# Neighbourhood attention in a hybrid encoder layer: the bias laid out beside the gates and kept in DRAM, and weight low parts, output sums and gate products on VectorE

## The chip, the cores and the metric

The kernel runs on one core of a Trainium2 chip. The metric is the device time of one execution in microseconds (us). A profiled execution gives the trace; its span is the time from the first to the last instruction. The engines are called TensorE (PE in the profile, with PEld for its weight loads), VectorE (DVE), ScalarE (ACT) and GpSimd (POOL). SP issues the DMAs.

## The reference, cut to what matters

One layer, 1024 tokens and 16 meta tokens, width 1024. A combined projection feeds two groups: latent attention (MLA) and two-dimensional neighbourhood attention (NA). NA has 16 heads of 64; a token on a 16 x 64 grid looks at a clamped 8 x 16 window, with a learned bias by relative offset, and at the 16 meta tokens, with a bias of their own.

```python
        k_win = k_rows[:, :, col_idx]
        v_win = v_rows[:, :, col_idx]
        dr_idx = r0 + jnp.arange(win_r, dtype=jnp.int32) - r + (NA_WIN_R - 1)
        bias = rel_bias[:, dr_idx[None, :, None], dc_idx[:, None, :]]
        s_win = (jnp.einsum('bqhd,brqchd->bhqrc', q_row, k_win).astype(jnp.float32) * scale
                 + bias.astype(jnp.float32)[None])
        s_meta = jnp.einsum('bqhd,bmhd->bhqm', q_row, k_meta).astype(jnp.float32) * scale + meta_b
        s = jnp.concatenate([s_win.reshape(B, NA_HEADS, GRID_W, n_win), s_meta], axis=-1)
        p = jax.nn.softmax(s, axis=-1).astype(v.dtype)
...
        y_na = _na(na_q, na_k, na_v, na_q_norm_w[l], na_k_norm_w[l],
                   na_rel_bias[l], na_meta_bias[l]) * jax.nn.silu(g_na)
        h_res = h_res + jnp.concatenate([y_mla, y_na], axis=-1) @ w_out[l]
```

q and k are normalised by head before this (QK-norm).

## The kernel before, in words

A float32 operand x is held as two parts in the matmul's type, a high part (a cast by ScalarE, such as wnh or hT) and a low part (x minus the high part, such as wnl or hTl). A product is then three matmuls: high x high, high x low, low x high. The helper that makes a low part is `lo_of`, one line of it (L104) being the operation of all of them; `mm` (L107) is every matmul, `tr` (L110) every transpose on TensorE. `bank` hands out PSUM banks by tag; s and tr share four, acc and o have two each.

The work stands in five stages, by time of the span:

- 0 to 190 us: the gates. 16 blocks of 128 gate columns, each for two halves of the tokens; a gate is 24 matmuls of 128x512. Weights come in groups gr of three blocks (`g_load`), four tiles of 128x2x384, into six buffers; the low parts of a tile are two operations on POOL. After each of the six gates of gr 3, `bias_rows` makes up to three of the 16 grid rows of `base`, the bias before it is laid out by window: two matmuls (rbh and rbl are the parts of the bias table, selr a selection matrix) and one VectorE operation. base then goes to DRAM as base_d.
- 190 to about 700 us: NA, 8 pairs of heads (p), each in 8 steps (t) of 128 tokens. The loop over g runs the projection of step g + 6 (`part`, in three pieces), the transposes of q and k of step g + 3 (`na_tr`), scores of step g + 1 (`na_qk`), the transposes of the probabilities of step g (`na_ptr`), and the products with v of step g - 1 (`na_pv`). `na_meta` projects the meta tokens of a pair at its step t=0. After every second step `na_pv` adds up the two banks of outputs into y_na; after every fourth `na_sum` and `na_fin` divide by the softmax sums and multiply by the gate.
- Behind the last pair's projections the same loop runs the projection of the latent keys and values (`lat_nat`, natl), whose norm is on POOL.
- Up to 1160 us: MLA. Then the output projection.

TensorE runs in the order in which the code is written. The other queues (VectorE, ScalarE, POOL and SP) are put in order by a scheduler, so code that is moved can move instructions of all of them; within a queue, an instruction that waits holds all behind it.

QK-norm goes through `na_norm`: sums of squares, then `rstd`, in which POOL does a pow (L93) and VectorE one Newton step (L94, L95, L97), then raw x rs_y (L467). The transposes of `na_tr` read raw. `na_bias` loads a pair's base rows and lays them out as bi (inner steps), b0 and b7 (first and last step) with 11 operations, on POOL for p > 0. `na_load` loads a pair's weights; all eight low parts are on POOL for p > 0:

```python
        d["w"] = w_load(lambda k: w_na[p, :, 2 * k:2 * k + 2, :], 384, (G, G if p else V), True)
```

G, V, S and T are POOL, VectorE, ScalarE and TensorE. In the outputs ScalarE copies both halves out of PSUM (u_na and u2_na) and POOL adds them; rx, kvm and u2_na share one buffer (tag ux).

Of the kernel before, what the change touches and what calls it, by code (L numbers as in the profile page):

```python
# [48 lines left out]
def hybrid_layer(ctx, tc, x, x_t, meta, meta_t, norm_w, w_na, w_g, w_lat, lat_w, w_uq, w_ukv, vec128, qpe_w, kpe_w,  # L49
# [375 lines left out]
    def na_bias(p):
        d = st[p]
        E = G if p else V
        bs = np2.tile([P, 2, NB * ROWS], F32, name="bs", bufs=1)
        nc.sync.dma_start(bs, base_d[2 * p:2 * p + 2].rearrange("h p n -> p h n"))
        bi = np2.tile([P, 2, WI], F32, name="bi")  # L430
        b0 = np2.tile([P, 2, WE], F32, name="b0", bufs=1)
        b7 = np2.tile([P, 2, WE], F32, name="b7", bufs=1)
        mb = metab[:, 2 * p:2 * p + 2, :]
        im = imask[:, None, :].to_broadcast([P, 2, WI])
        E.tensor_copy(b0[:, :, 0:128], bs[:, :, 128:256])
        E.tensor_copy(b0[:, :, 128:144], mb)
        E.tensor_copy(b0[:, :, 144:272], bs[:, :, 256:384])
        for o, bb, w in ((0, 0, 128), (144, 8, 128), (288, 16, 112)):
            E.tensor_tensor(bi[:, :, o:o + w], bs[:, :, bb * 16:bb * 16 + w], im[:, :, o:o + w], op=ALU.add)
        E.memset(bi[:, :, 128:144], MASK)  # L440
        E.tensor_copy(bi[:, :, 272:288], mb)
        E.tensor_copy(b7[:, :, 0:128], bs[:, :, 0:128])
        E.tensor_copy(b7[:, :, 128:144], mb)
        E.tensor_copy(b7[:, :, 144:272], bs[:, :, 128:256])
        d["bi"], d["b0"], d["b7"] = bi, b0, b7
# [849 lines left out]
```

## Time and profile before

| | us |
|---|---|
| median of 3 runs | 1372.32 (1371.27 to 1373.38) |
| the profiled execution's own time | 1372.07 |
| its span | 1370.3 |
| busy TensorE / VectorE / ScalarE / POOL in the span | 1310.3 / 924.6 / 833.7 / 568.5 |

TensorE is busy 96% of the span, but a busy TensorE is not always at full clock, and the share is an average over stages. The granted clock is 0.985 on average. Pairs are told apart by the first matmul of a pair's meta projection; pair 1 starts at 232.27 us, pair 6 at 532.28.

### The profile page before, as it was taken

How to read it: one execution, taken by the hardware profiler on the slowest of the kernel's cores; microseconds unless marked ns; L12 is line 12 of the kernel's file. 1: busy time of each engine (PE TensorE's matmuls, PEld its weight loads, DVE VectorE, ACT ScalarE, POOL GpSimd, SP SyncE). 2: the span in 40 equal slices, each digit the busy share in tenths (PEclk: the TensorE clock that was granted, in tenths of full speed). 3: DMA queues.
4: the chain of work that ended last, by engine and by line, in shares of the span. 5: the costliest groups of instructions: out<-in, count | busy, mean ns of one | idle time of the engine just before them, and what ended most of it. 6: DMA issues, size and time to landing. Idle time of an engine off the chain costs nothing.

```text
span 1370.3 us, 24834 instructions
## 1 busy us (share of the span) xinstructions
PE 1310.3 (96%) x8116; PEld 1212.9 (89%) x8116; DVE 924.6 (67%) x2957; ACT 833.7 (61%) x2319; POOL 568.5 (41%) x1057
## 2 busy tenths in 40 slices
PE   9999999999999989999789789999999999999999
PEld 7888889989898988999789789999999999988887
DVE  4923236877877877788648898988997998641110
ACT  6622136778787877788756567777777777630110
POOL 4312145465654746364445545724734652000000
PEclk9999999999999999999999899999999999999999
DMA  9342551221212213120201110100010022254231
GB/s 341 124 141 87 182 149 38 57 84 43 74 51 66 62 55 99 45 67 28 59 16 48 43 36 17 40 28 21 33 31 25 30 80 75 81 166 130 73 109 46
DMA packets 81968, 102.03 MB, mean 74 GB/s; under 512 B 10279, under 2 KB 60839, under 8 KB 81719
## 3 DMA queue, kind: packets, MB, share of 16 engines
q1 hardware_dynamic: 81839, 100.45, 23.4%
q8 instruction: 64, 1.05, 0.3%
q14 instruction: 65, 0.53, 0.1%
HBM read 70.01 MB, written 24.12 MB: 69 GB/s over the span
## 4 chain that ended last, share of the span: by engine, by line
PE 74%; DVE 14%; ACT 6%; issue 3%; POOL 2%; DMA 1%; SPq 0%; DVEq 0%; ACTq 0%; POOLq 0%
PE ps_acc L107 21%; PE mps_acc L107 11%; PE ps_s L107 9%; PE mps_s L107 8%; PE mps_st L107 7%; PE mps_o L107 5%; PE ps_o L107 5%; PE mps_tr L110 4%; PE ps_tr L110 4%; DVE m_sb L967 1%; DVE rs_y L97 1%; DVE rs_t L95 1%; DVE PT L104 1%; DVE mPT L104 1%; DVE rs_t L94 1%
## 5 line engine op out<-in xcount | busy, mean ns | idle before, releaser
L107 PE MATMUL ps_acc<-wnh,hT 128*128 128x384 f32 (+1 forms) x560 | 205.0, 366 | 6.0 <-DVE natl L666 5.5
L107 PE MATMUL ps_acc<-wnh,hTl 128*128 128x384 f32 (+1 forms) x560 | 188.8, 337 | 0.0
L107 PE MATMUL ps_acc<-wnl,hT 128*128 128x384 f32 (+1 forms) x560 | 188.5, 337 | 0.0
L93 POOL TENSOR_TENSOR rs_y<-rs_v,mhalf 128x1 f32<-128x1 f32 (+5 forms) x170 | 148.7, 878 | 75.2 <-DVE rs_v L89 52.9
L104 POOL TENSOR_TENSOR wnl<-wnf,wnh 128x384 fp32r<-128x384 f32 (+3 forms) x132 | 122.7, 954 | 104.9 <-ACT wnh L151 85.9
L107 PE MATMUL mps_s<-mkT,mq 128*128 128x346 f32 (+1 forms) x576 | 132.2, 338 | 1.3 <-DVE mPT L104 0.9
L107 PEld LDWEIGHTS ps_acc<-wnh,hT 128*128 128x128 f32 x560 | 107.2, 191 | 7.8 <-DVE natl L666 6.0
L561 ACT ACTIVATE s_sb<-s_sb,nmn 128x400 f32<-128x400 f32 (+1 forms) x128 | 77.0, 602 | 55.2 <-DVE nmn L559 54.5
L107 PEld LDWEIGHTS ps_acc<-wnl,hT 128*128 128x128 f32 x560 | 107.4, 192 | 0.0
L993 ACT CAST mPT<-mps_tr 128x512 fp32r<-128x512 f32 x128 | 74.5, 584 | 54.1 <-PE mps_tr L110 53.1
L107 PEld LDWEIGHTS ps_acc<-wnh,hTl 128*128 128x128 f32 x560 | 106.5, 190 | 0.0
L107 PE MATMUL mps_o<-mPT,mV 128*128 128x256 f32 x768 | 106.1, 287 | 0.0
L967 DVE TENSOR_SCALAR_CACHE_REDUCE m_sb<-mps_s 128x346 f32<-128x346 f32 (+1 forms) x192 | 97.4, 512 | 9.6 <-PE mps_s L107 7.7
L104 DVE TENSOR_TENSOR mPT<-mps_tr,mPT 128x512 fp32r<-128x512 f32 x128 | 87.6, 686 | 13.2 <-ACT mPT L993 12.0
L107 PEld LDWEIGHTS mps_s<-mkT,mq 128*128 128x128 f32 x576 | 93.4, 192 | 3.0 <-DVE mPT L104 1.5
L107 PEld LDWEIGHTS mps_o<-mPT,mV 128*128 128x128 f32 x768 | 94.8, 189 | 0.2
L530 POOL CAST qs<-qz 64x128 fp32r<-64x128 f32 x128 | 40.5, 316 | 124.9 <-ACT qz L526 88.9
L104 DVE TENSOR_TENSOR PT<-ps_tr,PT 128x384 fp32r<-128x384 f32 (+2 forms) x160 | 72.3, 469 | 24.1 <-ACT PT L582 23.3
L976 ACT ACTIVATE m_sb<-m_sb,mnm 128x1040 f32<-128x1040 f32 x64 | 74.6, 1166 | 19.8 <-DVE mnm L975 14.0
L110 PE MATMUL mps_tr<-ident,m_sb 128*128 128x128 f32 x512 | 76.7, 273 | 2.4 <-DVE mq L104 1.0
L582 ACT CAST PT<-ps_tr 128x384 fp32r<-128x384 f32 (+2 forms) x160 | 61.7, 407 | 17.4 <-PE ps_tr L110 16.5
L107 PE MATMUL ps_o<-PT,Vt 128*128 128x256 f32 x256 | 61.4, 301 | 8.2 <-DVE PT L104 7.8
(465 smaller groups left out, 3815.9 us busy)
## 6 DMA issues: line engine op xcount, KB each, us to landing
wnf<-in_w_na_dram SPq DMA_DIRECT2D x32, 384.0 KB, 3.5
g_d<-g SPq DMA_DIRECT2D x32, 256.0 KB, 2.3
wnf<-in_w_out_dram SPq DMA_DIRECT2D x32, 256.0 KB, 2.7
wnf<-in_w_g_dram SPq DMA_DIRECT2D x19, 384.0 KB, 4.7
Vp<-Vt SPq DMA_DIRECT2D x48, 112.0 KB, 2.2
yfo<-y_d SPq DMA_DIRECT2D x24, 192.0 KB, 2.7
gt<-g_d SPq DMA_DIRECT2D x16, 256.0 KB, 3.5
y_d<-y_na SPq DMA_DIRECT2D x16, 256.0 KB, 2.2
```

Source lines behind the costliest of these rows:

```text
L93: G.tensor_tensor(y, v, mhalf[:np_, :n], op=ALU.pow)
L94: E.tensor_tensor(t, y, y, op=ALU.mult)
L95: E.tensor_tensor(t, t, v, op=ALU.mult)
L104: eng.tensor_tensor(dst, src, f(hi), op=ALU.subtract)
L107: T.matmul(o, lhsT=l, rhs=r, start=start, stop=stop, skip_group_check=True)
L110: T.transpose(out=o, in_=i, identity=ident[: i.shape[0], : i.shape[0]])
L530: G.tensor_copy(qs[h_, j], qz[l_, j])
L561: S.activation(sb, sb, AF.Exp, scale=-1.0, bias=mn, accum_out=d["sum", t // 4][:, t % 4, j:j + 1])
L582: S.copy(pt[:n, c0:c1, 0, :], ps[:n, c0:c1])
L967: V.tensor_scalar(st["sb", h, t][:, ks], s_ps, -SCALE, BIG, op0=ALU.mult, op1=ALU.min, accum_out=st["mx", h, t][:, b:b + 1])
L976: S.activation(sb, sb, AF.Exp, scale=-1.0, bias=nm, accum_out=st["ms", h, t // 2][:, t % 2:t % 2 + 1])
L993: S.copy(dh, ps)
```

## The change

Five things are changed.

1. The bias matmuls stand behind the gates of gr 2 instead of gr 3. A new `stage_bias` lays the bias of one pair out, on POOL, after each of the first eight gates of gr 3 and later, and stores it in DRAM (bias_d). In NA one load by pair (bo) replaces `na_bias`'s load and its 11 operations. The mask and the meta bias are loaded early.
2. The low parts of the weights of pairs 1 to 7 are made by VectorE, not POOL.
3. The output sums: ScalarE copies one half (u_na), VectorE adds the other half out of PSUM. The copies u2_na and POOL's sum are gone. rx, now with a buffer of its own, is copied by ScalarE.
4. The product of gate and softmax reciprocal (gt) is on VectorE.
5. `na_meta` stands at t=1 (before: t=0) and `na_meta_tr` at t=3 (before: t=2).

```diff
     for gr in range(2, 6):
         gw = g_load(gr)
         for b in range(min(3, 16 - 3 * gr)):
             for hf in (1, 0):
                 gate(3 * gr + b, gw, b * P, hf)
-                if gr == 3:
+                if gr == 2:
                     for k in range(3):
                         rk = (2 * b + hf) * 3 + k
                         if rk < ROWS:
                             bias_rows(rk)
-        if gr == 3:
-            nc.sync.dma_start(base_d.rearrange("h p n -> p h n"), base.rearrange("p h b r -> p h (b r)"))
-            sctx.close()
+                elif todo_b:
+                    stage_bias(todo_b.pop(0))
+    sctx.close()
...
+    def stage_bias(p):
+
+        E = G
+        bs = base[:, 2 * p:2 * p + 2].rearrange("p h b r -> p h (b r)")
+        bo = sg.tile([P, 2, WB], F32, name="sgb", bufs=3)
+        bi, b0, b7 = bo[:, :, :WI], bo[:, :, WI:WI + WE], bo[:, :, WI + WE:]
+        mb = metab[:, 2 * p:2 * p + 2, :]
+        im = imask[:, None, :].to_broadcast([P, 2, WI])
+        for o, bb, w in ((0, 0, 128), (144, 8, 128), (288, 16, 112)):
+            E.tensor_tensor(bi[:, :, o:o + w], bs[:, :, bb * 16:bb * 16 + w], im[:, :, o:o + w], op=ALU.add)
+        E.memset(bi[:, :, 128:144], MASK)
+        E.tensor_copy(bi[:, :, 272:288], mb)
+        for b_, c in ((b0, 128), (b7, 0)):
+            E.tensor_copy(b_[:, :, 0:128], bs[:, :, c:c + 128])
+            E.tensor_copy(b_[:, :, 128:144], mb)
+            E.tensor_copy(b_[:, :, 144:272], bs[:, :, c + 128:c + 256])
+        nc.sync.dma_start(bias_d[p], bo)
...
     def na_load(p):
         d = st[p] = {}
-        d["w"] = w_load(lambda k: w_na[p, :, 2 * k:2 * k + 2, :], 384, (G, G if p else V), True)
+        d["w"] = w_load(lambda k: w_na[p, :, 2 * k:2 * k + 2, :], 384, (V, V) if p else (G, V), True)
...
+        bo = np2.tile([P, 2, WB], F32, name="bo")
+        nc.sync.dma_start(bo, bias_d[p])
+        st[p].update(bi=bo[:, :, :WI], b0=bo[:, :, WI:WI + WE], b7=bo[:, :, WI + WE:])
...
                 o = d["o"][j].rearrange("p t (a n) -> p t a n", a=2)
                 S.copy(u[a], o[b])
-                S.copy(u2[a], o[a])
-            G.tensor_tensor(u, u, u2, op=ALU.add)
...
+                V.tensor_tensor(u[a], u[a], o[a], op=ALU.add)
+            V.tensor_tensor(y, u[:, :, 0, :], u[:, :, 1, :], op=ALU.add)
...
-        rx = np2.tile([P, 4, 2, 64], F32, name="rx", tag="ux", bufs=1)
-        G.tensor_copy(rx.rearrange("p t j d -> p (t j) d"),
-                      r.rearrange("p t j -> p (t j)")[:, :, None].to_broadcast([P, 8, 64]))
+        rx = np2.tile([P, 4, 2, 64], F32, name="rx", bufs=1)
+        S.copy(rx.rearrange("p t j d -> p (t j) d"),
+               r.rearrange("p t j -> p (t j)")[:, :, None].to_broadcast([P, 8, 64]))
...
-        G.tensor_tensor(gt, gt, rp, op=ALU.mult)
+        V.tensor_tensor(gt, gt, rp, op=ALU.mult)
...
             if t == 0:
+                na_alloc(p)
+            if t == 1:
                 na_meta(p)
...
-            if t == 2:
+            if t == 3:
                 na_meta_tr(p)
```

How this moves instructions is shown at three places. The first is TensorE's queue around the first gate of gr 2. ps_acc and ps_s are the PSUM banks of two gates, hT and hTl the parts of the normed tokens (92 and 94 the second half of the tokens, 91 and 93 the first), wnh and wnl those of the weights. Before, the gate's last matmuls are followed by the next gate:

```order
L107 MATMUL ps_acc<-hT_92,wnh 128x512
L107 MATMUL ps_acc<-hTl_94,wnh 128x512
L107 MATMUL ps_acc<-hT_92,wnl 128x512 [waits Pool_49]
L107 MATMUL ps_s<-hT_91,wnh 128x512 [waits PE_49,Activation_49]
L107 MATMUL ps_s<-hTl_93,wnh 128x512
```

In the changed kernel six bias matmuls stand between them:

```order
L108 MATMUL ps_acc<-hT_92,wnh 128x512
L108 MATMUL ps_acc<-hTl_94,wnh 128x512
L108 MATMUL ps_acc<-hT_92,wnl 128x512 [waits Pool_49]
L108 MATMUL ps_tr<-rbh,selr 128x384 [waits DMAHW3_49,DMAHW2_49,DMAHW4_49,DMAHW1_49,DMAHW5_49,DMAHW0_49,DMAHW6_49,DVE_49,DMAHW7_49,PE_49,Activation_49]
L108 MATMUL ps_tr<-rbl,selr 128x384 [waits DVE_49]
L108 MATMUL ps_o<-rbh,selr 128x384
```

The bias matmuls, with their waits for the table's loads and parts, have come forward by six gates, from behind the first gate of gr 3.

The second place is VectorE's queue in a pair of NA, from the Newton step of raw to the low parts of the next pair's weights. PT are the transposed probabilities, Vt the parts of v, bi the bias of an inner step, s_sb the scores. Before (a pair's steps t=1 and 2):

```order
L464 TENSOR_REDUCE ssn<-sqn 128x8
L104 TENSOR_TENSOR Vt<-ps_acc,Vt 128x128
L89 TENSOR_SCALAR rs_v<-ssn 128x8
L104 TENSOR_TENSOR kM<-ps_tr,kM 64x128 x2
L529 SCALAR_TENSOR_TENSOR qs<-ps_tr,qkw_na,qz_1618 64x128 x2
L94 TENSOR_TENSOR rs_t<-rs_y 128x8
L559 ISA s_sb,nmn<-ps_s,b_3905 128x272
```

In the changed kernel, the piece with two of the eight low parts of a pair:

```order
L96 TENSOR_TENSOR rs_t<-rs_t,rs_v 128x8
L105 TENSOR_TENSOR wnl<-wnf,wnh 128x384
L105 TENSOR_TENSOR PT_1737<-ps_tr,PT_1737 128x3x128
L105 TENSOR_TENSOR wnl<-wnf,wnh 128x384
L105 TENSOR_TENSOR PT_1739<-ps_tr,PT_1739 128x3x128
L620 TENSOR_TENSOR y_na<-u_na 128x256
L98 SCALAR_TENSOR_TENSOR rs_y<-rs_t,rs_y 128x8
L105 TENSOR_TENSOR kM<-ps_tr,kM 64x128 x2
```

The low parts (wnl) now stand between operations that TensorE waits for: PT, and the Newton step before raw.

The third place is POOL's queue in the gates. Before, twelve low parts of 128x384 (gr 3 and 4) and eight of 128x128 (gr 5) follow one another:

```order
L93 TENSOR_TENSOR rs_y<-rs_v,mhalf 128x1 x4
L93 TENSOR_TENSOR rs_y<-rs_v,mhalf 16x1
L104 TENSOR_TENSOR wnl<-wnf,wnh 128x384 x8
L349 TENSOR_TENSOR tabq<-cs,qpw 128x8x32 x4
L349 TENSOR_TENSOR tabk<-csm,kpw 16x32 x4
L349 TENSOR_TENSOR tabk<-cs,kpw 128x8x32 x4
L104 TENSOR_TENSOR wnl<-wnf,wnh 128x384 x12
L104 TENSOR_TENSOR wnl<-wnf,wnh 128x128 x8
```

In the changed kernel the last tile of gr 4 stands in the middle of the eighth bias block (sgb):

```order
L398 TENSOR_TENSOR sgb<-base,imask 128x2x128 x2
L398 TENSOR_TENSOR sgb<-base,imask 128x2x112
L399 MEMSET sgb 128x2x16
L400 COPY sgb<-metab 128x2x16
L105 TENSOR_TENSOR wnl<-wnf,wnh 128x384 x2
L402 COPY sgb<-base 128x2x128
L403 COPY sgb<-metab 128x2x16
```

Six whole blocks stand ahead of the two middle tiles of gr 4, and one and a half more between these and its last tile, so these low parts have moved behind the bias.

## Rows read from the trace of the kernel before

**Rows 1.** Busy time by stretch: us, each engine, clock, DMA share, GB/s.

```profile
232.27:289.40 57.13, 56.09 (x365) 53.53 (x363) 45.01 (x133) 47.50 (x140) 33.77 (x48) 1.00 0.22 61
532.28:593.73 61.45, 57.60 (x364) 55.35 (x363) 48.21 (x134) 48.14 (x142) 33.80 (x49) 0.97 0.20 63
232.27:593.73 361.46, 342.15 (x2169) 327.80 (x2168) 285.38 (x803) 287.01 (x841) 204.92 (x288) 0.98 0.21 63
645.00:712.00 67.00, 54.08 (x337) 50.39 (x337) 37.74 (x118) 42.10 (x126) 31.82 (x75) 0.90 0.13 38
900.00:1000.00 100.00, 99.55 (x746) 97.77 (x745) 87.48 (x344) 74.11 (x211) 52.75 (x136) 1.00 0.09 29
```

**Rows 2.** TensorE's waits in NA: us in total, times, longest.

```profile
PE ps_tr L110 <- DVE nmn L559: 14.4, 6, 2.7
PE ps_acc L107 <- DVE natl L666: 5.5, 2, 4.3
PE ps_tr L110 <- POOL rx L622: 4.8, 1, 4.8
```

**Rows 3.** Timeline of pair 6: start us, us, operation, [idle before].

```profile
537.49 4.36 POOL L104 TENSOR_TENSOR wnl<-wnf,wnh 128x384 fp32r<-128x384 f32 x4
539.53 1.47 DVE L467 TENSOR_TENSOR raw<-raw,rs_y 128x512 f32<-128x512 f32 x1
543.33 0.44 PE L110 MATMUL ps_tr<-ident,raw 128*128 128x128 f32 x2 [2.66 <-DVE nmn L559]
547.17 0.52 PE L107 MATMUL ps_acc<-wnh,hTl 128*128 128x384 f32 x1
```

**Rows 4.** VectorE's timeline in pair 5.

```profile
497.07 0.17 DVE L97 SCALAR_TENSOR_TENSOR rs_y<-rs_t,rs_y 128x8 f32<-128x8 f32 x1
498.01 0.69 DVE L467 TENSOR_TENSOR raw<-raw,rs_y 128x512 f32<-128x512 f32 x1
```

**Rows 5.** VectorE's groups in pair 5: busy us, mean ns, idle before.

```profile
L467 DVE TENSOR_TENSOR raw<-raw,rs_y 128x512 f32<-128x512 f32 x4 | 3.8, 949 | 0.1
L97 DVE SCALAR_TENSOR_TENSOR rs_y<-rs_t,rs_y 128x8 f32<-128x8 f32 x4 | 3.0, 744 | 0.1
L95 DVE TENSOR_TENSOR rs_t<-rs_t,rs_v 128x8 f32<-128x8 f32 x4 | 2.7, 666 | 0.1
L94 DVE TENSOR_TENSOR rs_t<-rs_y 128x8 f32<-128x8 f32 x4 | 1.7, 416 | 0.7 <-POOL rs_y L93 0.7
```

**Rows 6.** VectorE's groups in the whole span.

```profile
L104 DVE TENSOR_TENSOR y0l<-yf,y0h 128x384 fp32r<-128x384 f32 x4 | 2.1, 555 | 0.2 <-ACT y0h L940 0.2
L104 DVE TENSOR_TENSOR mPT<-mps_tr,mPT 128x512 fp32r<-128x512 f32 x128 | 87.6, 686 | 13.2 <-ACT mPT L993 12.0
```

**Rows 7.** Timeline of the end of NA.

```profile
701.18 1.26 POOL L608 TENSOR_TENSOR u_na<-u_na 128x512 f32<-128x512 f32 x1
```

**Rows 8.** Timeline in gr 2.

```profile
81.06 0.39 PE L107 MATMUL ps_s<-hT,wnh 128*128 128x512 f32 x1
86.50 0.39 PE L107 MATMUL ps_acc<-hT,wnh 128*128 128x512 f32 x1
88.56 0.56 DVE L104 TENSOR_TENSOR rbl<-rb,rbh 120x384 fp32r<-120x384 f32 x1 [2.50 <-ACT rbh L341]
```

**Rows 9.** POOL's groups in pair 5; timeline at gr 4's start.

```profile
L439 POOL TENSOR_TENSOR bi<-bs,imask 128x256 f32<-128x256 f32 x2 | 1.4, 731 | 0.0
L442 POOL COPY b<-bs 128x256 f32<-128x256 f32 x1 | 0.4, 412 | 0.0
...
146.70 0.39 PE L107 MATMUL ps_acc<-hT,wnh 128*128 128x512 f32 x1
148.22 0.88 DVE L379 TENSOR_SCALAR base<-ps_o,rmask 128x384 f32<-128x384 f32 x1
```

**Rows 10.** Timeline of POOL and VectorE in the MLA stage.

```profile
788.87 0.56 POOL L93 TENSOR_TENSOR rs_y<-rs_v,mhalf 128x1 f32<-128x1 f32 x1 [0.59 <-DVE rs_v L89]
788.90 0.43 DVE L871 TENSOR_TENSOR mqraw<-mqraw,rs_y 128x256 f32<-128x256 f32 x1
```

More of the change, by code (lines that the diff above doesn't have):

```diff
@@ L34 @@
 WE = 272
+WB = WI + 2 * WE
 KS = 144
@@ L74, in load_bc @@
         return t
-    base_d = dram.tile([16, P, NB * ROWS], F32, name="base_d")
+    bias_d = dram.tile([NPAIR, P, 2, WB], F32, name="bias_d")
     g_d = dram.tile([16, P, D], F32, name="g_d")
@@ L300, in hybrid_layer @@
         for b in range(3):
-            gs = gp.tile([P, 512], F32, name="gs", bufs=5)
+            gs = sp.tile([P, 512], F32, name="gs", bufs=5)
             S.copy(gs, acc[b])
@@ L379, in bias_rows @@
         V.tensor_scalar(base[:, :, :, rk], ps, -1.0, rmask[:, rk:rk + 1], op0=ALU.mult, op1=ALU.add)
+    sg = sctx.enter_context(tc.tile_pool(name="stg", bufs=1))
+    imask = load(c_imask, [P, WI], "imask", sp1)
+    metab = load_bc(meta_bias, 16 * NM, "metab", sp1).rearrange("p (h m) -> p h m", h=16)
+    G.tensor_scalar(metab, metab, -1.0, None, op0=ALU.mult)
+    def stage_bias(p):
[14 more added lines that the diff above has]
+        nc.sync.dma_start(bias_d[p], bo)
+    todo_b = list(range(NPAIR))
     for gr in range(2, 6):
@@ L399, in hybrid_layer @@
     np2 = nx.enter_context(tc.tile_pool(name="na2", bufs=2, reuse_waits="tile"))
-    imask = load(c_imask, [P, WI], "imask", np1)
-    metab = load_bc(meta_bias, 16 * NM, "metab", np1).rearrange("p (h m) -> p h m", h=16)
-    V.tensor_scalar(metab, metab, -1.0, None, op0=ALU.mult)
     naw = load(na_w, [P, 2], "naw", np1)
@@ L422, in na_load @@
         d = st[p] = {}
-        d["w"] = w_load(lambda k: w_na[p, :, 2 * k:2 * k + 2, :], 384, (G, G if p else V), True)
+        d["w"] = w_load(lambda k: w_na[p, :, 2 * k:2 * k + 2, :], 384, (V, V) if p else (G, V), True)
     def na_bias(p):
[L426 to L445, printed above, removed]
+        bo = np2.tile([P, 2, WB], F32, name="bo")
+        nc.sync.dma_start(bo, bias_d[p])
+        st[p].update(bi=bo[:, :, :WI], b0=bo[:, :, WI:WI + WE], b7=bo[:, :, WI + WE:])
     def v_split(dst, src, n):
@@ L479, in k_split, with na_alloc @@
             lo_of(slot(kM[l_, j]), ps[h_], slot(kM[h_, j]))
-    def na_meta(p):
+    def na_alloc(p):
         d = st[p]
@@ L484, in na_meta @@
         d["V"], d["q"], d["nat"] = {}, {}, {}
+    def na_meta(p):
+        d = st[p]
         acc = bank("acc")
         proj(acc[:, :256], NT, d["w"], 128, 384)
-        kv = np2.tile([P, 256], F32, name="kvm", tag="ux", bufs=1)[:NM]
+        kv = np2.tile([P, 256], F32, name="kvm", bufs=1)[:NM]
         meta_sum(kv, acc[:, :256])
@@ L599, in na_pv @@
         if i == 1:
+            if t % 4 == 1:
+                d["y", t // 4] = np2.tile([P, 4, P], F32, name="y_na")
+            y = d["y", t // 4][:, t % 4 - 1:t % 4 + 1]
             u = np2.tile([P, 2, 2, P], F32, name="u_na", bufs=1)
-            u2 = np2.tile([P, 2, 2, P], F32, name="u2_na", tag="ux", bufs=1)
             for j in range(2):
@@ L606, in na_pv @@
                 S.copy(u[a], o[b])
-                S.copy(u2[a], o[a])
-            G.tensor_tensor(u, u, u2, op=ALU.add)
-            if t % 4 == 1:
-                d["y", t // 4] = np2.tile([P, 4, P], F32, name="y_na")
-            V.tensor_tensor(d["y", t // 4][:, t % 4 - 1:t % 4 + 1], u[:, :, 0, :], u[:, :, 1, :], op=ALU.add)
+                V.tensor_tensor(u[a], u[a], o[a], op=ALU.add)
+            V.tensor_tensor(y, u[:, :, 0, :], u[:, :, 1, :], op=ALU.add)
     def na_sum(p, hf):
```

## The prediction

> **What bounds the kernel now.** I read the busy time by stage first, then TensorE's waits in the neighbourhood stage, then the timeline of one step, then the order of the changed kernel. Between 232.27 and 593.73 us stand pairs 1 to 6, 60.24 us each on average, and TensorE is busy 95% of that; VectorE 79% [rows 1]. So TensorE is the bound, but it loses time: pair 1 took 57.13 us with 1.04 us of idle TensorE at clock 1.00, pair 6 took 61.45 us with 3.85 us idle at clock 0.97. A stage of the MLA shows that VectorE can be busy 87.5% with TensorE at 99.5% [rows 1].
>
> The waits name where: 14.4 us in six waits for a transpose into ps_tr, 5.5 us for natl, 4.8 us for rx [rows 2]. The timeline of pair 6 shows the first kind. POOL runs four wnl parts, 4.36 us in a row; under them VectorE's raw x rs_y takes 1.47 us. Behind it in VectorE's queue stands L559, which takes the scores (and nmn) out of a bank that the next transpose needs, since s and tr share four; TensorE idles 2.66 us for it. Some 4 us later the 384-column matmuls take 0.52 us each [rows 3]: half clock for a stretch. At 0.97 of full clock on average, pair 6 lost 0.03 x 61.45 = 1.8 us by it [rows 1]. With POOL quiet the same raw operation takes 0.69 us and rs_y 0.17 [rows 4].
>
> **Part 1: less POOL in a pair.** The change takes wnl, u_na, gt, rx and the bias layout off POOL in pairs 1 to 7; what stays there is pow and the qs casts. By pair 5's groups, raw has a mean of 949 ns, the three small Newton operations 744, 666 and 416 ns [rows 5]. At 690 and 170 ns in quiet [rows 4], four of each give back 4 x (0.26 + 0.57 + 0.50 + 0.25) = 6.3 us of VectorE a pair.
>
> **Part 2: more VectorE in a pair.** Eight wnl of 128x384, eight sums u += o of 64x512 out of PSUM, two gt products of 128x512. Prices: 555 ns for a 384-wide difference in SBUF in quiet, 686 for a 512-wide one out of PSUM [rows 6]. Together 8 x 0.555 + 8 x 0.686 + 2 x 0.686 = 11.3 us. A wnl may cost more than 555: that is the low end, the high end is the 950 ns that raw has beside POOL [rows 5], +3.2 us a pair; I take the low end, since POOL is then quiet most of the time. VectorE comes to 48.2 - 6.3 + 11.3 = 53.2 us a pair. ScalarE, 48.1 us in pair 6 [rows 1], gives up eight copies of 64x512 and takes two of 128x512 (rx), so it falls. TensorE's matmuls are the same, 56.1 us by pair 1's busy figure (modelled ends, so rather too high), and remain the largest of the three.
>
> The pair then lies between pair 1's length, 57.1, and its TensorE floor without late operands, some 55.2 (pair 6's weight-load time, 55.35, is near it) [rows 1]; I take 56.3. That is the t0 wait (14.4 / 6 = 2.4) and the lost clock (1.8) gone from pair 6, less another 1 us of smaller waits. Moving the meta projection from t=0 to t=1 takes 16 small matmuls and the kvm work out of the step with the stall; I count it inside this. Gain: 6 x (60.24 - 56.3) = 23.6 us, and about 2.5 in pair 7 (one t0 wait).
>
> **Part 3: the end of the stage.** 4.3 us of the natl wait and 4.8 us for rx [rows 2] come from POOL's queue: rx stood behind u_na, 1.26 us long, on a buffer that it shared with u2 [rows 7]. Both leave POOL, and rx on ScalarE now stands ahead of the last u copies. The clock is 0.90 over these 67 us [rows 1], so up to 6.7 us are lost by it. I take 5.5 + 4.8 + 4.5 of the clock = 14.8, less 1.8 for the two or three sums of 0.686 [rows 6] that VectorE now does on the path there: 13 us.
>
> **Part 4: the bias matmuls come earlier.** In the changed order TensorE meets the first ps_tr<-rbh,selr right behind the first gate of gr 2. Before, that gate's last matmul was followed at 81.06 us by the next gate. The small parts rbl, which wait for the eight loads of rb and for the cast rbh, were ready at 88.56 + 0.56 = 89.12 [rows 8]. The queues of SP, ScalarE and VectorE up to there are the same after. So TensorE will wait 89.12 - 81.06 = 8.06 us; the clock after it costs 0 to the 1.8 of pair 6. I take 1.8, since the wait is longer than the 2.66 there: 9.9 us. Only if rbl were done by 81 would this be free, and nothing in the change moves its loads.
>
> **Part 5: POOL in the gates.** POOL lays the bias out between the wnl parts of gr 4. A block is three sums (up to 0.73 us), four wide copies (0.41) and four small operations at less than half of that [rows 9]: about 4.5 us. A lo part on POOL takes 4.36 / 4 = 1.1 us at most [rows 3]. gr 4 started at 146.70 us and base was complete 2.4 us later, at 149.10 [rows 9]; a gate takes 86.50 - 81.06 = 5.44 us [rows 8]. After, gr 4 starts at 146.70 + 9.9 = 156.6 and gr 3 six gates earlier, at 124.0, so base is complete at 126.4. Six blocks from there (the first has its small operations done: 26.3), two weight tiles (3.9), one and a half blocks (7.0) and the last tile's first lo part (1.0) end at 164.6. gr 4 wants that part three quarters through its first gate, with the third matmul there, at 156.6 + 4.1 + 0.4 = 161.1. Wait: 3.5 us (0 if POOL starts earlier, 8 if the loads queued behind the stores to bias_d are late).
>
> **The sum.** The profiled execution's own time is 1372.07, 0.25 below the runs' median. 1372.1 + 9.9 + 3.5 - 23.6 - 2.5 - 13 = 1346.4; with the 0.25 to the median I round to 1346. A change within 0.2%, 2.7 us, can't be told from none.
>
> **A rule to weigh.** POOL's pow of 0.56 us at 788.87 ran beside VectorE's 128x256 product of two SBUF operands, which took 0.43 from 788.90 on [rows 10], less than the 0.555 of a 384-wide one in quiet [rows 6], while wnl on POOL did lengthen such operations [rows 3]. The Trainium skill, "SBUF — State Buffer", section "Who interferes with whom", says that a VectorE operation with two SBUF inputs and a GpSimd operation that reads SBUF exclude one another for a whole instruction. The trace agrees for wnl and gt, and not for pow. By the rule the remaining POOL work would go on holding VectorE's new operations, which is rival (b) and its 1358; by the row at 788.90 the 1346 stand.
>
> **The rivals.**
> (a) VectorE becomes the bound. In pair 6 it was idle 61.45 - 48.21 = 13.2 us. If those waits stay while its work grows to 53.2, a pair takes 66.4; the NA stage gains nothing from 60.7 a pair on (waits of 7.5 us). Half-way, 63.5: 1372.1 + 13.4 + 6 x 3.3 - 13 = 1392. For it: 53.2 of 56.3 is 94%, above the 87.5% of any stage here. Against: its waits are for ScalarE and TensorE, and an engine that comes later finds its operands there. 0.12, on the slower side.
> (b) POOL's remaining pow and casts go on holding VectorE's operations of two SBUF operands. If half of the 6.3 us doesn't come back, VectorE has 53.2 + 3.2 = 56.4 us, as much as the pair; with the 2 us by which a pair then grows (half-way to 60.2) it is 1346 + 6 x 2 = 1358. For it: the raw row beside wnl; against: the row at 788.90, where pow holds nothing. 0.10.
> (c) Both early waits are hidden after all, because rbl's chain is done some 8 us sooner: 1346 - 9.9 - 3.5 = 1333. 0.08.
> (d) The gr 4 weights come 8 us later than the 3.5, behind the stores to bias_d on SP: 1354. 0.10.
> (e) The change doesn't do what it should in a pair: L559 stays as late, because the added lo parts and the kvm work stand ahead of it in place of the lengthened operations. Then pairs keep 60 us and only the end gains: 1372.1 + 13.4 - 13 = 1372. It decides once some 4 us (six added operations) stand ahead of one L559. 0.05.
>
> **How the numbers follow.** My forecast holds 0.55, from 1336 (a pair at 55.0) to 1356 (a pair at 57.5, early waits 3 us longer). The range takes in (b), (c), (d) and the forecast, with two in ten left for (a), (e) and mis-sizing: 1332 to 1366. Faster: 0.55 + 0.10 + 0.08 + 0.10, and a third of (a) where VectorE's waits shrink below 7.5, is 0.87; the same 0.04; slower 0.09.
>
> **What would show it.** TensorE's wait behind the first gate of gr 2, near 81 to 89 us, on rbl; one near 160 on wnl; no t0 wait over 1 us in pairs 1 to 7 and clock 1.00 there; raw at 0.69 us; no 4.8 us wait for rx. The prediction is wrong if TensorE waits on VectorE in most steps (a), or if raw and wnl on VectorE still take over 0.9 us (b).

## The result, and the profile after

The changed kernel takes 1396.45 us (median of 4 runs, 1395.56 to 1397.42) against 1372.85 before (1371.27 to 1373.94): a ratio of 1.0173, 95% interval 1.0155 to 1.0191. It is slower by 1.7%, where faster was forecast.

The page of the profile of the changed kernel, busy time by engine:

```profile
PE 1317.6 (94%) x8116; PEld 1215.9 (87%) x8116; DVE 951.3 (68%) x3081; ACT 810.2 (58%) x2271; POOL 441.5 (32%) x949
```

The work went where the change sends it: POOL lost 127 us, VectorE gained 27, ScalarE lost 24. The span grew by 24.3 us all the same, and TensorE idled in it.

Stretches of the changed kernel (columns as in [rows 1]): three in the gates, then pairs 1 to 6, then pair 6, each pair counted from the first projection matmul of its step 0:

```profile
88.30:92.00 3.70, 3.66 (x10) 3.07 (x11) 2.86 (x4) 0.00 (x0) 1.95 (x3) 0.50 0.51 173
164.00:168.00 4.00, 0.00 (x0) 0.00 (x0) 0.00 (x0) 0.74 (x2) 1.07 (x4) 0.70 0.97 322
168.00:172.00 4.00, 3.86 (x9) 2.70 (x10) 0.04 (x1) 0.99 (x3) 3.83 (x9) 0.50 0.38 146
250.94:627.74 376.80, 347.03 (x2170) 332.35 (x2168) 303.86 (x911) 269.48 (x803) 75.41 (x126) 0.96 0.23 69
565.04:627.74 62.70, 57.46 (x365) 55.04 (x363) 50.89 (x154) 45.05 (x134) 12.54 (x21) 0.97 0.23 71
```

A pair takes 62.8 us on average, where it took 60.2 [rows 1]. Where the 24.3 us are: up to step 0 of pair 1 +16.7 (250.94 against 234.23; 17.7 of it in the gates, with 1.0 back in pair 0), pairs 1 to 6 +15.4 (376.80 against 361.41), pair 7 up to its last step +4.3 (53.97 against 49.67), all behind it -12.1. The starts of the kernel before are counted in the same way from its trace.

TensorE's waits in the changed kernel (columns as in [rows 2]):

```profile
PE ps_acc L108 <- DVE nr L628: 19.5, 5, 3.9
PE ps_acc L108 <- ACT wnh L152: 7.5, 2, 7.1
PE ps_tr L108 <- ACT rbh L342: 6.5, 1, 6.5
PE ps_acc L108 <- DVE Vt L105: 5.9, 2, 3.2
PE ps_s L108 <- DVE kM L105: 4.9, 8, 1.8
```

The three kinds of wait of [rows 2] (ps_tr on nmn, natl, rx) are gone or down to 1.8 us; three others have come. The first and fourth line are one wait, seven times, once at the turn to each of pairs 1 to 7.

The two waits in the gates, in the timeline of the changed kernel (start, length, operation, idle before):

```profile
88.34 0.69 PE L108 MATMUL ps_tr<-rbh,selr 120*128 120x384 f32 x1 [6.48 <-ACT rbh L342]
...
158.77 0.87 SPq L405 DMA_DIRECT2D bias_d<-sgb  x2
159.75 2.38 SPq L142 DMA_DIRECT2D wnf<-in_w_g_dram  x2
167.26 1.14 ACT L152 CAST wnh<-wnf 128x768 fp32r<-128x768 f32 x2 [9.65 <-DMA wnf<-in_w_g_dram]
168.14 0.79 PE L108 MATMUL ps_acc<-hT,wnh 128*128 128x512 f32 x1 [7.09 <-ACT wnh L152]
```

The first is the forecast one: the bias matmuls stand ahead of their operands [rows 8]. The second is not a late low part but a late load: wnf is issued at 159.75, behind two stores to bias_d on SP, and is there at 167.26, while the DMA engines are busy 97% of the time. Behind each wait the granted clock is 0.50: from 88.34 to about 93.7 and from 168.14 to about 172.3 the matmuls of 128x512 follow one another every 0.43 us, where they do so every 0.23 us at full clock. That costs, by an estimate from these lengths, some 2.6 and 2.1 us more.

The wait at the turn of pair 6, in the same view:

```profile
570.53 0.68 DVE L643 TENSOR_TENSOR gt<-gt,nrp 128x512 f32<-128x512 f32 x1
571.32 0.68 DVE L619 TENSOR_TENSOR u_na<-u_na,ps_o 64x512 f32<-64x512 f32 x1
572.53 0.69 DVE L619 TENSOR_TENSOR u_na<-u_na,ps_o 64x512 f32<-64x512 f32 x1
573.25 0.69 DVE L644 SCALAR_TENSOR_TENSOR y_na<-y_na,gt 128x512 f32<-128x512 f32 x1
574.66 0.28 PE L108 MATMUL ps_acc<-wnl,hM 128*16 128x256 f32 x1
574.68 0.55 DVE L105 TENSOR_TENSOR wnl<-wnf,wnh 128x384 fp32r<-128x384 f32 x1
575.07 0.27 ACT L457 CAST Vt<-ps_acc 128x128 fp32r<-128x128 f32 x1
575.62 0.55 DVE L105 TENSOR_TENSOR wnl<-wnf,wnh 128x384 fp32r<-128x384 f32 x1
577.68 0.71 DVE L539 SCALAR_TENSOR_TENSOR qs<-ps_tr,qkw_na,qz 64x128 fp32r<-64x128 f32 x2
578.42 0.29 DVE L105 TENSOR_TENSOR Vt<-ps_acc,Vt 128x128 fp32r<-128x128 f32 x1
578.86 0.66 PE L108 MATMUL ps_acc<-wnh,hT 128*128 128x384 f32 x1 [3.93 <-DVE nr L628]
579.63 0.53 PE L108 MATMUL ps_acc<-wnh,hTl 128*128 128x384 f32 x1
```

The meta product (hM) ends at 574.66 + 0.28. The next matmul is the projection of step 1 and needs one of the two ps_acc banks. One holds the meta product, the other the projection of step 0, and the last reader of that is Vt on VectorE at 578.42. VectorE works without a gap from 570.53 on, and Vt stands behind all of the work shown. (The view names nr, which ends within 0.1 us of Vt; the experiments below decide between them.) Behind the wait matmuls take 0.53 us, half clock.

VectorE's groups between 300 and 580 us of the changed kernel (columns as in [rows 5]):

```profile
L105 DVE TENSOR_TENSOR wnl<-wnf,wnh 128x384 fp32r<-128x384 f32 x40 | 21.7, 552 | 1.4 <-ACT wnh L150 1.1
L474 DVE TENSOR_TENSOR raw<-raw,rs_y 128x512 f32<-128x512 f32 x18 | 12.3, 686 | 0.4
L98 DVE SCALAR_TENSOR_TENSOR rs_y<-rs_t,rs_y 128x8 f32<-128x8 f32 x18 | 3.0, 164 | 0.4
L619 DVE TENSOR_TENSOR u_na<-u_na,ps_o 64x512 f32<-64x512 f32 x36 | 24.7, 686 | 1.1
```

raw fell from 949 to 686 ns and rs_y from 744 to 164 [rows 5]; the new operations cost 552 and 686 ns. So the prices of the prediction are right, and the time went elsewhere.

### The profile page after: what moved, and what is told of

Its sections match the earlier page's. It is cut to its first block, busy times and chain, and to the rows that moved or that the text cites. A ratio compares the mean times of both kernels' runs of the same rounds, so it can differ in the third digit from the quotient of the medians.

```text
span 1394.6 us, 24728 instructions
## 1 busy us (share of the span) xinstructions
PE 1317.6 (94%) x8116; PEld 1215.9 (87%) x8116; DVE 951.3 (68%) x3081; ACT 810.2 (58%) x2271; POOL 441.5 (32%) x949
## 4 chain that ended last, share of the span: by engine, by line
PE 60%; DVE 22%; ACT 9%; DMA 3%; issue 3%; POOL 1%; SPq 0%; ACTq 0%; DVEq 0%; POOLq 0%
PE ps_acc L108 16%; PE mps_acc L108 9%; PE ps_s L108 7%; PE mps_s L108 7%; PE mps_st L108 6%; PE mps_o L108 4%; PE ps_o L108 4%; PE mps_tr L111 4%; DVE u_na L619 3%; PE ps_tr L111 2%; DVE qs L539 2%; ACT s_sb L571 2%; DVE m_sb L978 2%; DVE kM L105 2%; ACT qz L536 2%
## 5 line engine op out<-in xcount | busy, mean ns | idle before, releaser
L105 POOL TENSOR_TENSOR wnl<-wnf,wnh 128x384 fp32r<-128x384 f32 (+3 forms) x76 | 65.5, 880 | 92.3 <-ACT wnh L152 76.9
L569 DVE CUSTOM_DVE_ANT_0 s_sb<-ps_s,bo 128x400 f32<-128x400 f32 (+1 forms) x128 | 65.5, 531 | 6.1 <-PE ps_s L108 5.5
```

What stands on the lines that cost most here:

```text
L105: eng.tensor_tensor(dst, src, f(hi), op=ALU.subtract)
L569: V.tensor_tensor_reduce(out=sb, in0=s_ps, in1=bias[:, j, :], scale=1.0, scalar=BIG, op0=ALU.add, op1=ALU.min, accum_out=mn)
```

## The experiments

Ahead of each result stands what was expected before it ran, mostly as two rival theories, A and B. Most of these kernels were run once, and a single run is uncertain by some 4 us: one kernel gave 1360.4 the first time and 1354.3 to 1358.3 in four more runs. So the lengths of pairs 1 to 6 from the traces are read beside the times; in the one kernel that was traced twice (e5 and e13) they agree to 0.1 us (358.4). The kernel before, run beside them, took 1369.9 to 1374.9 (single runs, or medians where there are more).

**The meta projection back at t=0** (e1_meta_t0):

```diff
             if t == 0:
                 na_alloc(p)
-            if t == 1:
                 na_meta(p)
...
-            if t == 3:
+            if t == 2:
                 na_meta_tr(p)
```

> The changed kernel with the meta projection back at t=0 and its transposes back at t=2; all else as changed. Theory A (two PSUM banks for ps_acc: with the meta product ahead of step t=1, step 1's projection needs the bank of step 0, whose last reader, Vt on VectorE at 578.42 us, stands behind some 8 us of gt, output sums, wnl and PT): the 4.07 us wait in each of pairs 1 to 7 and the half clock after it (1.5 to 2.5) go, since step 0 then needs step 7's bank, read at a time when VectorE's queue is short; a pair falls from 62.8 to 57 to 59 us and the time by 25 to 40 us, to 1356 to 1371. Theory B (VectorE has simply too much work, 53 us in a pair, wherever the meta product stands): the wait turns up at another matmul and the time stays within 8 us of 1396.

1374.21 us, 22 less than the changed kernel and about the time of the kernel before (1374.87 beside it). The wait for the bank is gone but for one of 1.7 us at pair 7, and pairs 1 to 6 take 357.8 us in place of 376.8, at clock 1.00. Theory A holds in its mechanism; its length for a pair (57 to 59) was missed by 0.6 and its time (at most 1371) by 3, for the waits for PT come up instead (18.6 us in all, 6.1 in the changed kernel).

**The same move made in the kernel before** (e6_before_meta_t1), nothing else (na_alloc is the part of na_meta that hands out buffers, split off as in the changed kernel):

```diff
             if t == 0:
+                na_alloc(p)
+            if t == 1:
                 na_meta(p)
...
-            if t == 2:
+            if t == 3:
                 na_meta_tr(p)
```

> The kernel before with one edit: the meta projection at t=1 and its transposes at t=3; all VectorE work as before. Theory A (the bank rule makes step 1's projection wait for Vt of step 0 whatever VectorE does, and the queue there decides how long; before, POOL's work lengthens that queue): a wait of 1 to 4 us at the first projection matmul of t=1 in each pair, the 2.7 us wait at t=0 gone; the time between 1372 and 1385. Theory B (the place of the meta product is harmless without the added VectorE work): no wait there over 0.5 us and 1372 or less.

1384.17 us against 1371.89 for the kernel before. TensorE's waits in this kernel:

```profile
PE ps_acc L107 <- DVE Vt L104: 24.8, 7, 3.6
PE ps_o L107 <- DVE PT L104: 11.3, 9, 1.9
```

The move alone makes the wait, seven times, 3.5 us each, with POOL and VectorE as they were. Pairs 1 to 6 take 371.2 us, 9.8 more. Theory A.

**The bias matmuls behind the second to fifth gates of gr 2** (e2_shift):

```diff
-                    for k in range(3):
-                        rk = (2 * b + hf) * 3 + k
-                        if rk < ROWS:
-                            bias_rows(rk)
+                    gi = 2 * b + 1 - hf
+                    for rk in range(4 * gi - 4, min(4 * gi, ROWS)) if gi else ():
+                        bias_rows(rk)
```

> The changed kernel with the bias matmuls behind the second to fifth gates of gr 2, four grid rows each, in place of three behind each of the six. Theory A (TensorE waits 6.48 us at 88 us for rbh and rbl alone, and half clock costs 1.7 more): minus 8 us, 1388, with no wait over 1 us between 75 and 115 us. Theory B (the four rows find no PSUM banks, since VectorE needs 0.88 us for each and ps_tr and ps_o have two each): waits of 1 to 2 us at each of the four gates take the gain back, 1392 to 1396.

1397.18 us, no gain in the time. In the trace the wait for rbh falls from 6.5 to 2.1 us and step 0 of pair 1 comes 6.1 us earlier (244.88); behind pair 7 the same trace is 5.4 us longer than that of the changed kernel (718.2 from its last step to the end, 712.9 there), with a wait of 3.9 us for mq in the MLA stage that the kernel before has too. So theory A holds for the place, though 2.1 us of the wait remain, and not for the time; one run doesn't tell whether that later loss is the edit's.

**The low parts of the gates' weights of gr 3 to 5 on VectorE** (e3_gate_lo_v):

```diff
-        gw = g_load(gr)
+        gw = g_load(gr, (V, V) if gr > 2 else (G, G))
```

> The changed kernel with the low parts of the gates' weights of gr 3 to 5 on VectorE in place of POOL. Theory A (the last tile of gr 4 is late, 7.09 us at 168 us, because its load can't start until POOL has made low parts behind six bias blocks, and stands on SP behind the stores to bias_d): the wait goes, with the half clock after it minus 8 to 9 us, 1388. Theory B (the load is late because the DMA engines are 82% busy with the stores between 160 and 180 us): the wait stays over 4 us, 1392 to 1397.

1393.02 us. The wait of 7.1 us is gone from the list; step 0 of pair 0 starts at 199.3 us in place of 209.8. That is theory A for the wait. With the low parts on VectorE the last two tiles of gr 4 are loaded from 126.97 on, ahead of the first store to bias_d (130.55), and are 3.1 to 3.2 us on their way. In the changed kernel POOL makes the low parts ahead of the late load only behind six bias blocks, until 155.64; then SP stands at the store of a gate (g_d) until 158.36, and two bias stores go first. The late load is 7.4 us on its way while the DMA engines are full. e3 takes the load out of that stretch, so it shows that the late issue is needed for the wait, and not that the full engines add nothing. Of the time, pair 0 gives 4 us back (45.2 us in place of 41.1; one wait of 2.2 us for Vt), and 3.3 us more are lost from pair 7 on, so 3.4 us are left of the 8 to 9 of theory A.

**The low parts of pairs 1 to 7 back on POOL** (e4_wnl_pool):

```diff
-        d["w"] = w_load(lambda k: w_na[p, :, 2 * k:2 * k + 2, :], 384, (V, V) if p else (G, V), True)
+        d["w"] = w_load(lambda k: w_na[p, :, 2 * k:2 * k + 2, :], 384, (G, G) if p else (G, V), True)
```

> The changed kernel with the eight low parts of the weights of pairs 1 to 7 back on POOL. Theory A (the wait for Vt at t=1 is as long as VectorE's queue there, of which two or three wnl of 0.55 us are part, but wnl on POOL lengthens VectorE's operations of two SBUF operands under it again): the wait shrinks from 4.1 to 2 to 4 us, and the time by 0 to 12 us. Theory B (the eight wnl are what makes VectorE too slow): the wait goes and the time falls by over 20 us.

1386.30 us, pairs 1 to 6 at 361.8; the wait for Vt is 17.9 us in seven, 2.6 each. The queue ahead of Vt gets shorter, the wait remains: theory A.

**The three waits out at once** (e5_three_mended: the edits of e1 and e3, and the bias matmuls behind the third to sixth gates of gr 2, in the diff; e13_mended_timed is the same kernel, run four more times):

```diff
+                    gi = 2 * b + 1 - hf
+                    for rk in range(4 * gi - 8, 4 * gi - 4) if gi > 1 else ():
+                        bias_rows(rk)
```

> The changed kernel with three of its waits taken out at once: meta projection back at t=0, the bias matmuls behind the third to sixth gates of gr 2 (four grid rows each), the low parts of the gates' weights of gr 3 to 5 on VectorE. Theory A (the loss is the sum of three separate waits): from the 1374 of the kernel with the meta projection alone put back, minus 8 for the first gate wait and minus 8 for the second, 1356 to 1360, faster than the kernel before by 1%. Theory B (pair 0 gives back what the gates gain, since its own first loads come late, as it took 45.2 us in place of 41.1 with the gates' low parts alone moved): 1364 to 1370.

> The kernel with the three waits taken out, timed in five rounds: 1358 to 1363, a ratio of 0.989 to 0.994 to the kernel before, if the one look at 1360 holds; 0.995 to 1.000 if that look was a lucky one.

The first run took 1360.38; the four runs of e13 1356.32 us (1354.29 to 1358.26) against 1369.87, a ratio of 0.9906, interval 0.9889 to 0.9922. Step 0 of pair 1 comes 16.0 us earlier than in the changed kernel, and pairs 1 to 6 are 18.4 us shorter (19.0 in e1 alone): the losses in the gates and in the pairs were separate, and without them the change is a gain. But a pair still takes 59.7 us. Pairs 1 to 6 of e5, and TensorE's longest waits up to 730 us:

```profile
234.91:593.33 358.42, 339.53 (x2168) 322.69 (x2166) 300.15 (x911) 271.28 (x807) 77.22 (x127) 1.00 0.24 73
...
PE ps_tr L111 <- DVE PT L105: 9.7, 13, 1.6
PE ps_o L108 <- DVE PT L105: 8.6, 15, 1.7
```

VectorE is busy 84% there, 50.0 us a pair, TensorE 95%; yet 18 us of waits (15 of them in pairs 1 to 6) are for PT, a product of VectorE. At the turn to pair 6, where VectorE works without a gap, PT stands behind gt and two output sums:

```profile
535.67 0.69 DVE L642 TENSOR_TENSOR gt<-gt,nrp 128x512 f32<-128x512 f32 x1
...
538.42 1.39 DVE L618 TENSOR_TENSOR u_na<-u_na,ps_o 64x512 f32<-64x512 f32 x2
539.84 0.56 DVE L105 TENSOR_TENSOR PT<-ps_tr,PT 128x384 fp32r<-128x384 f32 x1
540.46 0.44 PE L111 MATMUL ps_tr<-ident,raw 128*128 128x128 f32 x2 [1.53 <-DVE PT L105]
```

**Low parts half and wholly on POOL, from there** (e7_mended_half_pool with `(G, V)`, e8_mended_wnl_pool with `(G, G)`):

> The kernel with the three waits taken out, and of the eight weight low parts of a pair four on POOL and four on VectorE. Theory A (what is left in a pair, 59.6 us against TensorE's 55 to 56, is VectorE's queue: PT comes late): four wnl less give 2.2 us of VectorE back and POOL's four lengthen fewer operations than the eight before did: a pair at 58 to 59 us, 4 to 8 us faster than with all eight on VectorE. Theory B (each wnl on POOL costs VectorE as much in lengthened operations as it saves): within 3 us of it.

> The kernel with the three waits taken out, and all eight weight low parts of a pair on POOL, as before the change. Theory A (VectorE's queue is the bound in a pair): 4.4 us of VectorE back, some 3 to 4 lost again to lengthened operations: 0 to 6 us faster than with all eight on VectorE. Theory B (lengthened operations cost more than the work saved): slower than it by 3 to 8 us.

1366.87 and 1365.04 us: 6.5 and 4.7 us above e5. Pairs 1 to 6 take 362.5 and 359.5, 4.1 and 1.1 more. With half of them on POOL the bank wait is back (17.1 us in eight), now at step 0; with all of them the wait for nmn is (11.1 us in six), as in [rows 2]. Theory A is out for both: giving low parts to POOL shortened no pair. With half of them the kernel lost more than theory B has (3 us); with all, the time fits theory B, but 1.1 us in six pairs hardly tell it from none.

**The gt products back on POOL, from there** (e10_gt_pool):

```diff
-        V.tensor_tensor(gt, gt, rp, op=ALU.mult)
+        G.tensor_tensor(gt, gt, rp, op=ALU.mult)
```

> The kernel with the three waits taken out, and the two gt products of a pair back on POOL. Theory A (at the turn of a pair VectorE's queue, into which the gt product falls, holds PT and so TensorE): 2 x 0.69 us less on VectorE in a pair, half of them at the turn; the pair shortens by 0.3 to 0.7 us, 2 to 5 us in all, unless POOL's 1.3 us product lengthens rs_t and u sums under it by as much. Theory B (it does): within 2 us of 1360.

1367.91 us, pairs 1 to 6 at 366.6 (clock 0.96). Both theories are wrong: taking 1.4 us a pair off VectorE cost 8 us. In the trace, most of the 1.4 us comes back at once, for a wnl of VectorE beside POOL's product takes 1.57 us in place of 0.56:

```profile
541.58 1.29 POOL L642 TENSOR_TENSOR gt<-gt,nrp 128x512 f32<-128x512 f32 x1 [0.19 <-ACT nrp L636]
541.72 1.57 DVE L105 TENSOR_TENSOR wnl<-wnf,wnh 128x384 fp32r<-128x384 f32 x1
547.59 0.44 PE L111 MATMUL ps_tr<-ident,raw 128*128 128x128 f32 x2 [2.13 <-DVE PT L105]
```

VectorE's order changes too: raw (0.69 us) now stands ahead of the PT that TensorE wants. The waits for PT into ps_tr are then 11.0 us in five, 2.1 to 2.4 each, where they were 9.7 in 13, 1.6 at most. The sum of the waits has hardly grown, but at each of these five turns the granted clock is 0.50 for 3.4 to 6.8 us, where e5 has one such stretch in pairs 1 to 6: TensorE is busy 346.4 us in them in place of 339.5, and that is 6.9 of the 8.2 us.

**The output sums back on ScalarE and POOL, from there** (e11_sum_pool; rx stays on ScalarE but shares a buffer with u2 and kvm again):

```diff
+            u2 = np2.tile([P, 2, 2, P], F32, name="u2_na", tag="ux", bufs=1)
...
                 S.copy(u[a], o[b])
-                V.tensor_tensor(u[a], u[a], o[a], op=ALU.add)
+                S.copy(u2[a], o[a])
+            G.tensor_tensor(u, u, u2, op=ALU.add)
```

> The kernel with the three waits taken out, and the output sums as before the change (eight copies more on ScalarE, the 1.3 us sum on POOL, u2, kvm and rx in one buffer again; rx stays on ScalarE). Theory A (the sums cost VectorE 5.5 us a pair and are the largest part of its new work): a pair falls from 59.7 to 57 to 58.5 us, but the end of the stage gets back the waits for rx and natl: 1352 to 1360. Theory B (the POOL sum lengthens VectorE's operations under it and u2's buffer delays rx): 1360 to 1368.

1352.07 us, pairs 1 to 6 at 346.5: 57.8 us a pair. Its stretch, and TensorE's longest waits up to 730 us:

```profile
234.62:581.12 346.50, 335.71 (x2168) 320.71 (x2166) 282.03 (x862) 293.44 (x851) 107.67 (x150) 1.00 0.25 75
...
PE ps_o L108 <- ACT u_na L619: 6.8, 5, 1.4
PE ps_tr L111 <- ACT rx L632: 4.5, 1, 4.5
PE ps_o L108 <- DVE PT L105: 3.6, 3, 1.4
```

The waits for PT fall from 18.3 to 3.6 us. ScalarE has 3.7 us a pair more, and TensorE waits for it 6.8 us. Theory A; and the wait for rx is back, as expected.

**The same with rx in nrp's buffer** (e14_best):

```diff
-        rx = np2.tile([P, 4, 2, 64], F32, name="rx", tag="ux", bufs=1)
+        rx = np2.tile([P, 4, 2, 64], F32, name="rx", tag="rxp", bufs=1)
...
+        rp = d["rp"] = np2.tile([P, 512], F32, name="nrp", tag="rxp", bufs=1)
```

> The kernel with the three waits taken out and the output sums back on ScalarE and POOL, rx in one buffer with nrp, so that it no longer waits for u2. Theory A (the 4.5 us wait for rx at the end of the stage, in the look with rx, u2 and kvm in one buffer, comes from that buffer): it goes, minus 4 to 7 us with the clock: 1345 to 1349, a ratio of 0.981 to 0.985. Theory B (rx waits for ScalarE's queue there, not for the buffer): the wait stays, 1350 to 1354.

1351.62 us (1350.11 to 1353.05) against 1371.16: a ratio of 0.9855, interval 0.9838 to 0.9873, the fastest of the kernels here. The wait for rx is gone, so it was the buffer; but pairs 1 to 6 take 350.9 in place of 346.5, so the time didn't follow: theory A for the wait, while the time lies where theory B had it, and not for theory B's reason. Why the pairs grew is open.

**Low parts on VectorE in the kernel before, alone** (e12_before_wnl_v: `(V, V) if p else (G, V)`):

> The kernel before with one edit: the eight weight low parts of pairs 1 to 7 on VectorE; sums, gt, rx, bias layout and meta projection as before. Theory A (lengthened operations were worth at most as much as the 4.4 us of work that replaces them): VectorE's raw falls to about 0.7 us, the 2.7 us wait at t=0 shrinks by less than 1 us; 1368 to 1376. Theory B (the lengthening by wnl was the cause of that wait, as the prediction had it): the wait and the half clock after it go, 1345 to 1360.

1367.47 us against 1369.87; pairs 1 to 6 at 356.7, 4.7 less. The wait for nmn is gone from the list, as theory B has it, and the clock is 1.00; the time is 0.5 below the range of theory A, for the waits for PT rise from 7.8 to 13.3 us (9.8 and 3.5). rs_y still has a mean of 508 ns: u_na and gt stay on POOL, and in the trace the long ones stand beside POOL's sum (0.97 us at 506.29, beside u_na from 505.94 on).

**The changed kernel with the old sums alone** (e15_after_sum_pool, the sums' diff of above):

> The changed kernel with the output sums as before the change (ScalarE and POOL; u2, kvm and rx in one buffer), the meta projection at t=1 as changed. Theory A (the 4.07 us wait for Vt at t=1 is as long as VectorE's queue between 570 and 578 us, of which the two sums of 0.69 are part, and POOL's sum replaces them at no cost to VectorE): the wait falls to 2 to 3 us, the pair from 62.8 to 60 to 61, 1378 to 1388. Theory B (the sums hold VectorE only by their own time, elsewhere in the pair): the wait stays at 4 us and the time falls by less than 6 us.

1391.09 us, pairs 1 to 6 at 369.5, 7.3 less. The wait for Vt stays, 26.9 us in seven. In pair 6:

```profile
565.75 1.29 POOL L621 TENSOR_TENSOR u_na<-u_na 128x512 f32<-128x512 f32 x1 [1.98 <-ACT u_na L620]
565.89 1.70 DVE L646 SCALAR_TENSOR_TENSOR y_na<-y_na,gt 128x512 f32<-128x512 f32 x1
572.03 0.29 DVE L105 TENSOR_TENSOR Vt<-ps_acc,Vt 128x128 fp32r<-128x128 f32 x1
572.47 0.66 PE L108 MATMUL ps_acc<-wnh,hT 128*128 128x384 f32 x1 [4.19 <-DVE Vt L105]
```

Here nr stands well ahead of Vt and the view names Vt itself: the wait is Vt's. It is as long as before. Two sums of 0.69 are gone, but y_na beside POOL's sum takes 1.70 us in place of 0.69, so 1.0 of the 1.4 us comes back; the rest was not followed. Theory B's numbers hold, though by this lengthening, which theory B doesn't name.

**Only the bias layout left of the change** (e16_bias_only: three waits out; low parts, sums and gt on POOL; rx on ScalarE):

> The kernel with the three waits taken out, and weight low parts, output sums and gt product all back on POOL (rx on ScalarE): of the change, the bias layout beside the gates remains, in NA one load in place of 11 POOL operations. Theory A (the bias layout, 5 us of POOL a pair that mostly falls into quiet places, was not what lengthened VectorE's operations at t=0): the 2.7 us wait at t=0 stays and a pair is at 59.5 to 60.5 us; 1362 to 1370. Theory B (the bias layout was what pushed wnl and gt under VectorE's raw chain): the wait goes and a pair falls below 58.5.

1368.04 us against 1371.16, pairs 1 to 6 at 358.0, 3.4 less than before. The wait for nmn is there again (12.3 us in five). Theory A.

## Why the prediction was wrong

1. **The bound and the first wait.** Right: L559 stood behind operations that POOL's work had lengthened; with wnl moved (alone, in e12) the wait for nmn goes, and raw falls from a mean of 0.93 us to 0.73 (300 to 580 us).
2. **The prices.** Right: 552 ns for wnl, 686 for a sum, 0.69 for gt. VectorE's 53.2 us a pair came out as 50.9, ScalarE fell to 45.1.
3. **"Moving the meta projection from t=0 to t=1 ... I count it inside this".** This step failed, and it is the largest loss: the prediction put the move at nothing, and with it undone (e1) the kernel is back at the time of the kernel before. It was read as less work in the step with the stall. The order was not followed to the banks: the meta product takes one ps_acc bank and step 1 then needs the one whose last reader stands at the end of VectorE's queue. At t=0 the same rule holds for step 7's bank, but Vt was done there at 533.36 (533.08 + 0.28), before TensorE came for the bank at 534.19. Timeline of the kernel before:

```profile
533.08 0.28 DVE L104 TENSOR_TENSOR Vt<-ps_acc,Vt 128x128 fp32r<-128x128 f32 x1
534.19 0.34 PE L107 MATMUL ps_acc<-wnh,hT 128*128 128x384 f32 x1
```

The runs: the move costs 9.8 us in pairs 1 to 6 of the kernel before (e6), and 19.0 there in the changed one, with 5.0 more in pair 7 (e1).
4. **"I take 56.3".** Mis-sized too: with the meta product back a pair is 59.6 us. The sum of VectorE, below TensorE's, was taken to mean that its work is covered. gt, sums and wnl of a pair fall together around the turn to the next, where VectorE works without a gap while PT, which TensorE wants, stands in the queue (timeline of e5). Of the three only the sums were shown to be the cost: without them on VectorE a pair is 57.8 (e11), where the prediction's upper end for a pair was 57.5, while wnl (e7, e8) or gt (e10) put back on POOL made no pair shorter. Rival (a) named the right engine with the wrong measure: VectorE is at 81% in pair 6 and its order, not its sum, decides. TensorE waits for the bank once in a pair, not in most steps, so it is luck that rival (a)'s 1392 lies near the measured time.
5. **The end of the stage, 13 us.** The size came out, in part by luck: from the last step of pair 7 to the first mps_o matmul it is 131.2 us in place of 144.0, 12.8 less. rx is free as forecast (4.8 us), but of the natl wait of 5.5 us 1.8 stay. A wait of 3.9 us for mq, in the MLA part of this stretch, which the prediction doesn't have, is gone in the changed kernel. It is there again in e2 and e4, whose code is that of the changed kernel from here on, and the stretch then takes 137.7 and 138.6 us. With this wait on both sides the gain is 6.2 and 5.3 us, not 13; why the wait comes and goes is open.
6. **The bias matmuls, 9.9 us.** Right in place and mechanism: 6.48 us of wait in place of 8.06, and 2.6 of half clock in place of 1.8: 9.1. The wait is shorter since it ends with rbh, which the first matmul reads, and not with rbl.
7. **POOL in the gates, 3.5 us.** This step failed too: 7.09 us and 2.1 of half clock, 9.2. The prediction took POOL's queue to end at 164.6 with the tile's low part; in the trace POOL stands idle for 3.10 us before that low part, which begins at 168.17, as the tile isn't loaded. Rival (d) had the place: the load stands behind the stores to bias_d.

By stretches the errors add to the difference. The prediction had -26.1 us for pairs 1 to 7, and +19.7 came (15.4 + 4.3); it had +13.4 for the gates, and +16.7 came up to pair 1; it had -13 behind, and -12.1 came. 45.8 + 3.3 + 0.9 = 50.0 is what separates 1346.4 from 1396.4. Of the 45.8, 24.0 go when the meta projection is put back (19.0 + 5.0, e1): that is step 3, by one run. The other 21.8 are step 4.

## What to carry to other kernels

When a matmul group is moved, count PSUM banks at its new place: which earlier result must have been read out before the next group may start, by which engine, and what stands ahead of that reader in its queue. An engine whose sum in a period is below the bound can still hold it, if the added work falls together at one place; read the fullest steps, not the sum. Here new stores and new work on POOL made a load leave late, beside full DMA engines; moving the work that held the load (the low parts, to a VectorE with time to spare) was enough.

## What the runs showed of the hardware

A wnl on VectorE beside POOL's pow, in the changed kernel:

```profile
567.27 1.64 POOL L94 TENSOR_TENSOR rs_y<-rs_v,mhalf 128x8 f32<-128x8 f32 x1 [6.44 <-DVE rs_v L90]
567.46 0.56 DVE L105 TENSOR_TENSOR wnl<-wnf,wnh 128x384 fp32r<-128x384 f32 x1 [0.33 <-ACT wnh L150]
```

It starts 0.19 us into the pow, which goes on until 568.91, and takes its 0.56 us. The same two meet in pairs 1 to 5: in four of them the wnl starts 0.09 to 0.12 us into the pow and takes 0.56 us; in pair 3 it starts first (377.46, the pow at 377.48), and the pow takes 2.04 us in place of 1.64. POOL's sum of 1.29 us did lengthen y_na (to 1.70, above), and its product of 1.29 us a wnl (to 1.57, in e10). The Trainium skill, "SBUF — State Buffer", section "Who interferes with whom", has an operation of VectorE with two SBUF inputs wait for a whole GpSimd instruction that reads SBUF. The traces agree for sums and products over 512 columns, and not for this pow once it has begun.
